# Where tiles lie in a partition: permanent tiles and weights at the upper end, the down projection's moving operands behind the tokens' tiles

## The chip, the cores and the metric

The kernel runs on one core of one Trainium2 chip. The metric is device time in microseconds (us) of one execution, lower is better. The kernel before has a median of 1196.31 us over 3 runs (1194.72 to 1197.14).

A core has five engines that run side by side. TensorE (PE) multiplies matrices: it loads a 128x128 *stationary* operand into its array (a weight load, "PEld" in the profile) and then streams a *moving* operand of up to 512 columns past it (a matmul, "PE"). VectorE (DVE) and ScalarE (ACT) do elementwise work, GpSimd (POOL) a few memsets, SyncE (SP) issues the transfers (DMA). All of them work on the on-chip memory SBUF: 128 partitions, each a line of bytes. A tile of 128x512 float32 takes 2,048 bytes of every partition. Matmul results go to a second memory, PSUM, in banks of 512 float32.

## The reference

Two layers of a token trunk, 512 tokens of width 1024. Each layer adds a mixer's output and then a gated MLP with a causal convolution of width 3. What matters here is the size and the order of the products:

```python
for i in range(DEPTH):                                  # 2 layers
    h = rms_norm(x, attn_norm[i])
    proj = h @ w_in[i]                                  # differential attention, then GLA
    mix = diff_attention(...) if i % 2 == 0 else gla_attention(...)
    cross = memory_cross_attention(mem_q, mem, ...)     # into 256 memory tokens
    x = x + concat([mix, cross]) @ w_out[i]
    h = rms_norm(x, ffn_norm[i])
    x = x + conv_ffn(h, w_up[i], conv_w[i], conv_b[i], w_down[i])

def conv_ffn(h, w_up, conv_w, conv_b, w_down):
    u = h @ w_up                                        # 1024 -> 5632
    c = causal_depthwise_conv(u, conv_w) + conv_b
    a, g = split(c, 2)
    return (silu(g) * a) @ w_down                       # 2816 -> 1024
```

## The kernel before, in words

**Products.** Every large product is done in three float32r matmuls: an operand is split into a high part and a low part, and high x high, high x low and low x high are summed in one PSUM bank. Two helpers do this. `gemm` (lines 244 to 264, matmuls on lines 255 to 257) makes tokens-by-features results: the tokens' tiles are stationary, the *weights* are the moving operand, 512 columns at a time (272 and 256 for two of the pieces). `product` (lines 267 to 274, matmuls on lines 272 to 274) makes features-by-tokens results: 128 columns of the weights are stationary and the *tokens'* tile of 512 columns is the moving operand. The output projection, the up projection and the down projection go through `product`. With a call to each matmul there is one weight load; it runs while the matmul before it streams.

**Order.** The order on PE is the program's own (line 141: the PE part of the schedule is manual). The other engines' orders come from the framework's planner, which also places every semaphore. Products of the projections are cut into units and handed out between the attention's steps by the `Filler` class, by estimated cost. Weights arrive through `make_piece` (line 214): a transfer of up to 128x1024 float32 into a `raw` tile, then ACT copies it to `whi` and DVE subtracts it into `wlo`.

**The MLP.** `ffn` (lines 1011 to 1078) works in two halves of 12 and 10 groups of 128 channels. For each group: the up projection of both gate sides (`up`, line 1018) into PSUM banks "mm" and "sm", a scaling into one of four tiles `u` (line 1026), three convolution steps into a tile `cvo` (lines 1028 to 1030), a gate, and a split into a high and a low tile (lines 1058 to 1061). The first 5 groups of a half put these two tiles among the tokens' tiles (`xs`), the other 7 or 5 into slots of their own with the tag "mid" (18 slots), called `midh` and `midl` in the profile. The down projection (lines 1066 to 1076) then runs `product` over all groups of the half, once for each of eight blocks of 128 output channels, into banks "lg" and "tp". Its moving operands are thus five pairs of `xs` tiles, then seven (or five) pairs of `mid` tiles.

**Pools and places.** Tiles come from pools. A pool takes one stretch of the partition, its size rounded to 32 bytes; with no side named, pools stack upward from the lower end, and a pool that is closed gives its stretch to the next one. A tile that reuses bytes waits until the readers of the tile before it are done. From the program before, in bytes of a partition:

| pool | holds | from | to |
| --- | --- | --- | --- |
| (reserved) | scratch of the transfers, four constants | 0 | 16,512 |
| `perm` | constants, norm gains, memory keys and values | 16,512 | 31,112 |
| `xs` | 36 slots of 2,048: tokens' tiles and most temporaries | 31,136 | 104,864 |
| `wp` | 3 slots `raw`, 5 `whi`, 5 `wlo`, 4,096 each | 104,864 | 158,112 |
| `cp` | small vectors, 64 bytes a slot | 158,112 | 162,208 |
| `at0` | layer 0's attention | 162,208 | 207,264 |
| `ff0`, `ff1` | `rB`, `u`, `cvo`, then the 18 `mid` slots from 184,864 on | 162,208 | 221,728 |
| `at1` | layer 1's attention | 162,208 | 228,128 |

`at0`, `ff0`, `at1` and `ff1` follow one another on the same bytes. Lines 135 to 138 open the permanent pools, lines 1082 and 1091 the four that alternate.

Of the kernel before, what the change touches and what calls it, by code (L numbers as in the profile page):

```python
# [129 lines left out]
def trunk(ctx, tc, head_d, x_t, mem_t, wpack, cols_a_d, cols_d, conv_d, gate_d, rel_bias, diff_lambda, consts, onehot, out):  # L130
# [1 line left out]
    mm = nc.tensor.matmul  # L132
    V, A, G = nc.vector, nc.scalar, nc.gpsimd

    perm = ctx.enter_context(tc.tile_pool(name="perm", bufs=1))
    xs = ctx.enter_context(tc.tile_pool(name="xs", bufs=1))
    wp = ctx.enter_context(tc.tile_pool(name="wp", bufs=2))
    cp = ctx.enter_context(tc.tile_pool(name="cp", bufs=4))
    ps = ctx.enter_context(tc.tile_pool(name="ps", bufs=2, space=PSUM))
    dr = ctx.enter_context(tc.tile_pool(name="dr", bufs=1, space=DRAM))  # L140
    ctx.enter_context(tc.manual_schedule(engines={mybir.EngineType.PE}))
# [1 line left out]
    def bank(tag):  # L143
        return ps.tile([128, 512], F32, name=f"ps_{tag}", tag=tag)

    def xtile():
        return xs.tile([128, S], F32, name="xt", tag="xs", bufs=XS)

    def split_tiles(pool=None, tag="xs", bufs=XS):
        pool = pool or xs  # L150
        return (pool.tile([128, S], F32R, name=tag + "h", tag=tag, bufs=bufs),
                pool.tile([128, S], F32R, name=tag + "l", tag=tag, bufs=bufs))
# [19 lines left out]
    def tables(name):  # L172
        tc.keep_in_program_order(A.preload_act_table_set(name))


    def newton(v, y, t):
        V.tensor_mul(t, y, y)
        V.scalar_tensor_tensor(t, t, -0.5, v, op0=ALU.mult, op1=ALU.mult)
        V.scalar_tensor_tensor(y, t, 1.5, y, op0=ALU.add, op1=ALU.mult)
# [48 lines left out]
    def weights(key):  # L228
        i = used[0]
        assert plan[i][0] == key, (plan[i][0], key)  # L230
        while len(made) < min(i + 2, len(plan)):
            make_piece()
        used[0] += 1
        parts, made[i] = made[i], None
        return parts
# [31 lines left out]
    def product(p, parts, n, pairs, ids=None):  # L267
        ids = range(len(parts)) if ids is None else ids
        first, last = (ids[0], ids[-1]) if len(ids) == len(parts) else (0, len(parts) - 1)
        for i in ids:  # L270
            (hi, lo), (bh, bl) = parts[i], pairs[i]
            mm(p, hi[:, blk(n)], bh, start=i == first, stop=False)  # L272
            mm(p, hi[:, blk(n)], bl, start=False, stop=False)  # L273
            mm(p, lo[:, blk(n)], bh, start=False, stop=i == last)  # L274
# [84 lines left out]
    with tc.tile_pool(name="ini", bufs=1) as ip, tc.manual_schedule(engines={E.Activation, E.DVE, E.Pool, E.SP}):  # L359
# [29 lines left out]
        parts, acc, split_w = [], [None], [None]  # L389
# [587 lines left out]
    def update(n, p, gain, acc):  # L977
        V.tensor_add(xT[n], xT[n], p)
        if gain is None:
            return  # L980
        xh[n], xl[n] = split_tiles()
        split(xh[n], xl[n], xT[n], gain(n))
        squares(xT[n], acc)


    def out_proj(l, mix, part, acc, late=None):
        got, kk = {}, dict(PASS[l][part])
        turns = cycle(("mm", "mm", "sm", "sm") if late is not None else ("mm", "sm") if acc else ("mm",))

        def unit(n, i):  # L990
            c, ks = n // 2, kk[n // 2]
            if i == 0:
                if c not in got:
                    got[c] = weights(("o", l, part, c))
                got["p", n] = bank(next(turns))
            p = got["p", n]
            product(p, got[c], n % 2, [mix[k] for k in ks], (i,))
            if i == len(ks) - 1:
                update(n, p, None if acc is None else (lambda k: c_ffn(l, k)), acc)

        def give(units):
            for u in units:
                F.add(0.65, lambda u=u: unit(*u))
        units = [(2 * c + n, i) for c, ks in PASS[l][part] for n in range(2) for i in range(len(ks))]
        if late is None:
            return give(units)
        early = [u for u in units if u[0] < 4 and kk[u[0] // 2][u[1]] != late]
        give([u for u in early if u[0] < 3])
        return lambda: give([u for u in early if u[0] == 3] + [u for u in units if u not in early])

    def ffn(pool, l, acc):
        rB = pool.tile([128, S], F32, name="rB", bufs=1)
        us = [pool.tile([128, S + 2], F32, name=f"u{i}", bufs=1) for i in range(4)]
        for u in us:
            G.memset(u[:, 0:2], 0.0)
        nu = [0]

        def up(parts, n):
            i = nu[0]
            nu[0] += 1  # L1020
            p = bank("mm" if i % 4 < 2 else "sm")
            product(p, parts, n, list(zip(xh, xl)))
            return p, us[i % 4]

        def conv(p, u, j):
            V.tensor_mul(u[:, 2:], p, rB)  # L1026
            c = pool.tile([128, S], F32, name="cvo", bufs=6)
            A.activation(c, u[:, 2:], AF.Identity, scale=cv[l][:, 2, j:j + 1], bias=cv[l][:, 3, j:j + 1])  # L1028
            V.scalar_tensor_tensor(c, u[:, 1:S + 1], cv[l][:, 1, j:j + 1], c, op0=ALU.mult, op1=ALU.add)  # L1029
            V.scalar_tensor_tensor(c, u[:, 0:S], cv[l][:, 0, j:j + 1], c, op0=ALU.mult, op1=ALU.add)  # L1030
            return c

        def row_scales(sq):
            p = bank("tp")
            mm(p, ones, sq, start=True, stop=True)
            v, t = xtile(), xtile()
            A.activation(rB, p, AF.Ln, scale=1.0 / D, bias=eps)
            V.tensor_scalar(v, p, 1.0 / D, EPS, op0=ALU.mult, op1=ALU.add)
            A.activation(rB, rB, AF.Exp, scale=-0.5)
            newton(v, rB, t)  # L1040

        base = 0
        for half, nq in enumerate(HALVES):
            mids = []
            for q in range(base, base + nq):
                wa = weights(("ua", l, q))
                wg = None
                for n in range(2):
                    ua = up(wa, n)
                    wg = wg or weights(("ug", l, q))  # L1050
                    if q == 0 and n == 0:
                        row_scales(acc[0])
                    ug = up(wg, n)
                    ca = conv(*ua, 2 * q + n)
                    cg = conv(*ug, 22 + 2 * q + n)
                    A.activation(cg, cg, AF.Silu)
                    V.tensor_mul(ca, ca, cg)
                    mh, ml = split_tiles() if len(mids) < 5 else split_tiles(pool, "mid", 18)
                    A.copy(mh, ca)
                    V.tensor_sub(ml, ca, mh.bitcast(F32))  # L1060
                    mids.append((mh, ml))
            last = half == 1
            if last and l == 0:
                tables("natural_log_exp_and_others")
            acc2 = [None]
            for c in range(4):
                pn = bank("lg"), bank("tp")
                parts = weights(("dn", l, base, c))
                for n in range(2):
                    product(pn[n], parts, n, mids)  # L1070
                for n in range(2):
                    update(2 * c + n, pn[n], (lambda k: c_attn(1, k)) if last and l == 0 else None, acc2)
                    if last and l == 0:
                        nc.sync.dma_start(xres[2 * c + n], xT[2 * c + n])
                    if last and l == 1:
                        nc.sync.dma_start(out[2 * c + n], xT[2 * c + n])
            base += nq
        return acc2

    acc = None  # L1080
    for l in range(2):
        with tc.tile_pool(name=f"at{l}", bufs=2) as pool:
            mix = [None] * 8
            sums, acc = acc, [None]
            if l == 0:
                diff_layer(pool, mix, acc)
            else:
                gla_layer(pool, mix, sums)
                out_proj(1, mix, len(PASS[1]) - 1, acc)
                F.flush()  # L1090
        with tc.tile_pool(name=f"ff{l}", bufs=2) as pool:
            acc = ffn(pool, l, acc)


def _constants():
# [72 lines left out]
```

## Time and profile before

| what | value |
| --- | --- |
| median of 3 runs (lowest, highest) | 1196.31 us (1194.72, 1197.14) |
| the profiled execution's own time | 1194.47 us |
| its span, first to last instruction | 1192.7 us |
| outside the span | 1.8 us |
| granted TensorE clock | 1.00 |
| ACT busy, DVE busy | 548.3 us, 760.1 us |
| DMA, mean over the span | 99 GB/s |

How to read it: a line of the grouped view gives the source line, the engine, the operation, the tile that is written, an arrow, and the tiles that are read; then the shapes, how many there were, their busy time together and the mean time of one in nanoseconds, and at last the idle time of the engine in front of them. For a matmul the first tile after the arrow is the moving operand and the second the stationary one. Matmuls are pipelined: one lasts longer than the distance to the next one's start, so the time that a matmul costs is the distance between starts, not its length. In a row of windows the count behind PE takes in matmuls that began before the window and still ran; the count behind PEld is that of the weight loads, one for each matmul begun.

### The profile page before, as it was taken

The numbers are of one execution on the slowest core, as the hardware profiler recorded it, in microseconds if no ns is written. First come the engines' busy times: TensorE is split into PE (matmuls) and PEld (weight loads), VectorE is DVE, ScalarE is ACT, GpSimd is POOL, SyncE is SP. The second block draws the span as 40 slices with busy tenths as digits, with TensorE's granted clock in tenths as the row PEclk, the third lists the DMA queues.
The fourth block names the chain that finished last, engine by engine and source line by source line (L and its number), as shares of the span: only waits on it lengthen the run. The fifth ranks groups of instructions, "written<-read, shape, count | busy, mean of one in ns | idle before, by whom it ended". The sixth has DMA issues, their size and how long they took to land.

```text
span 1192.7 us, 14774 instructions
## 1 busy us (share of the span) xinstructions
PE 1179.3 (99%) x5656; PEld 965.8 (81%) x5656; DVE 760.1 (64%) x1270; ACT 548.3 (46%) x966; POOL 4.5 (0%) x25
## 2 busy tenths in 40 slices
PE   9999998999999999999999999999999999999998
PEld 6887776788888888888888788987888888888887
DVE  7566587687767434767556746768777743476741
ACT  6676586564434223434436534436443422243420
POOL 0000000000000000000000000000000000000000
PEclk9999999999999999999999999999999999999999
DMA  8322214042322332322342221333233233242231
GB/s 296 124 96 81 80 55 141 27 136 76 116 96 86 109 107 71 123 71 89 117 144 78 72 71 58 103 104 125 73 109 103 81 114 106 71 124 72 89 115 44
DMA packets 39268, 117.81 MB, mean 99 GB/s; under 512 B 4671, under 2 KB 6520, under 8 KB 39198
## 3 DMA queue, kind: packets, MB, share of 16 engines
q1 hardware_dynamic: 39054, 116.62, 30.5%
q8 instruction: 44, 0.72, 0.3%
q10 hardware_dynamic: 144, 0.26, 0.1%
q14 instruction: 26, 0.21, 0.1%
HBM read 112.65 MB, written 4.21 MB: 98 GB/s over the span
## 4 chain that ended last, share of the span: by engine, by line
PE 93%; DVE 3%; ACT 2%; DMA 1%; issue 1%; SPq 0%; ACTq 0%; DVEq 0%
PE ps_mm L273 8%; PE ps_mm L274 8%; PE ps_mm L272 8%; PE ps_sm L274 7%; PE ps_sm L273 7%; PE ps_sm L272 7%; PE ps_mm L255 5%; PE ps_mm L257 5%; PE ps_mm L256 5%; PE ps_lg L273 3%; PE ps_lg L272 3%; PE ps_lg L274 3%; PE ps_tp L272 3%; PE ps_tp L273 3%; PE ps_tp L274 3%; PE ps_tp L170 2%
## 5 line engine op out<-in xcount | busy, mean ns | idle before, releaser
L201 ACT CAST whi<-raw 128x1024 fp32r<-128x1024 f32 (+4 forms) x212 | 208.5, 985 | 263.9 <-PE ps_tp L273 134.7
L204 DVE TENSOR_TENSOR wlo<-raw,whi 128x1024 fp32r<-128x1024 f32 (+4 forms) x212 | 241.3, 1140 | 117.1 <-ACT whi L201 116.4
L272 PE MATMUL ps_mm<-xsh,whi 128*128 128x512 f32 x446 | 176.4, 396 | 0.0
L273 PE MATMUL ps_mm<-xsl,whi 128*128 128x512 f32 x446 | 173.8, 390 | 0.2 <-DVE xsl L239 0.2
L274 PE MATMUL ps_mm<-xsh,wlo 128*128 128x512 f32 x446 | 173.7, 389 | 0.0
L272 PE MATMUL ps_sm<-xsh,whi 128*128 128x512 f32 x386 | 150.3, 389 | 0.0
L274 PE MATMUL ps_sm<-xsh,wlo 128*128 128x512 f32 x386 | 150.2, 389 | 0.0
L273 PE MATMUL ps_sm<-xsl,whi 128*128 128x512 f32 x386 | 150.2, 389 | 0.0
L255 PE MATMUL ps_mm<-whi,xsh 128*128 128x512 f32 (+2 forms) x352 | 136.9, 389 | 0.1
L257 PE MATMUL ps_mm<-whi,xsl 128*128 128x512 f32 (+2 forms) x352 | 131.1, 373 | 0.3 <-DVE xsl L239 0.3
L256 PE MATMUL ps_mm<-wlo,xsh 128*128 128x512 f32 (+2 forms) x352 | 130.6, 371 | 0.0
L1028 ACT ACTIVATE cvo<-u,cv 128x512 f32<-128x512 f32 x88 | 71.6, 814 | 121.4 <-DVE u L1026 121.4
L273 PEld LDWEIGHTS ps_mm<-xsl,whi 128*128 128x128 f32 x446 | 83.8, 188 | 17.8 <-DVE xsl L239 0.6
L272 PEld LDWEIGHTS ps_mm<-xsh,whi 128*128 128x128 f32 x446 | 83.8, 188 | 17.5 <-issue 0.8
L274 PEld LDWEIGHTS ps_mm<-xsh,wlo 128*128 128x128 f32 x446 | 83.7, 188 | 17.4
L1029 DVE SCALAR_TENSOR_TENSOR cvo<-u,cv,cvo 128x512 f32<-128x512 f32 x88 | 65.8, 748 | 38.7 <-ACT cvo L1028 38.7
L273 PEld LDWEIGHTS ps_sm<-xsl,whi 128*128 128x128 f32 x386 | 72.5, 188 | 15.1
L272 PEld LDWEIGHTS ps_sm<-xsh,whi 128*128 128x128 f32 x386 | 72.5, 188 | 15.0
L274 PEld LDWEIGHTS ps_sm<-xsh,wlo 128*128 128x128 f32 x386 | 72.5, 188 | 15.0
L255 PEld LDWEIGHTS ps_mm<-whi,xsh 128*128 128x128 f32 x352 | 66.3, 188 | 13.8 <-issue 3.4
L257 PEld LDWEIGHTS ps_mm<-whi,xsl 128*128 128x128 f32 x352 | 66.1, 188 | 12.6 <-DVE xsl L239 0.5
L256 PEld LDWEIGHTS ps_mm<-wlo,xsh 128*128 128x128 f32 x352 | 66.4, 189 | 9.7
(257 smaller groups left out, 1734.9 us busy)
## 6 DMA issues: line engine op xcount, KB each, us to landing
raw<-in_wpack_dram SPq DMA_DIRECT2D x178, 512.0 KB, 3.5
xt<-in_x_t_dram SPq DMA_DIRECT2D x15, 256.0 KB, 5.9
raw<-in_wpack_dram SPq DMA_DIRECT2D x15, 256.0 KB, 2.6
raw<-in_wpack_dram SPq DMA_DIRECT2D x8, 384.0 KB, 3.4
xres<-xt SPq DMA_DIRECT2D x8, 256.0 KB, 2.0
xt<-xres SPq DMA_DIRECT2D x8, 256.0 KB, 3.9
out_dram<-xt SPq DMA_DIRECT2D x8, 256.0 KB, 2.0
bt<-bias_d SPq DMA_DIRECT2D x6, 256.0 KB, 3.1
```

The source lines that it names most:

```text
L170: nc.tensor.transpose(dst, src, ident[:n, :n])
L201: ins = A.copy(hi[:, c], raw[:, c])
L204: V.tensor_sub(lo[:, c], raw[:, c], hi[:, c].bitcast(F32))
L255: mm(p, sh[k][:, blk(b)], hi, start=k == 0, stop=False)
L256: mm(p, sh[k][:, blk(b)], lo, start=False, stop=False)
L257: mm(p, sl[k][:, blk(b)], hi, start=False, stop=k == KT - 1)
L272: mm(p, hi[:, blk(n)], bh, start=i == first, stop=False)
L273: mm(p, hi[:, blk(n)], bl, start=False, stop=False)
L274: mm(p, lo[:, blk(n)], bh, start=False, stop=i == last)
L1028: A.activation(c, u[:, 2:], AF.Identity, scale=cv[l][:, 2, j:j + 1], bias=cv[l][:, 3, j:j + 1])
L1029: V.scalar_tensor_tensor(c, u[:, 1:S + 1], cv[l][:, 1, j:j + 1], c, op0=ALU.mult, op1=ALU.add)
```

## The change

The pools `perm`, `wp` and `cp` are opened on the right side: they stack downward from the upper end of the partition. `xs` and the attention's pools stay on the left. The MLP's pool is divided: the `mid` slots get a pool of their own on the left, the rest (`rB`, `u`, `cvo`) a pool on the right. No instruction is added, removed or put in another place of the program.

```diff
-    perm = ctx.enter_context(tc.tile_pool(name="perm", bufs=1))
+    perm = ctx.enter_context(tc.tile_pool(name="perm", bufs=1, side="right"))
     xs = ctx.enter_context(tc.tile_pool(name="xs", bufs=1))
-    wp = ctx.enter_context(tc.tile_pool(name="wp", bufs=2))
-    cp = ctx.enter_context(tc.tile_pool(name="cp", bufs=4))
+    wp = ctx.enter_context(tc.tile_pool(name="wp", bufs=2, side="right"))
+    cp = ctx.enter_context(tc.tile_pool(name="cp", bufs=4, side="right"))
...
-    def ffn(pool, l, acc):
+    def ffn(mid, pool, l, acc):
...
-                    mh, ml = split_tiles() if len(mids) < 5 else split_tiles(pool, "mid", 18)
+                    mh, ml = split_tiles() if len(mids) < 5 else split_tiles(mid, "mid", 18)
...
-        with tc.tile_pool(name=f"ff{l}", bufs=2) as pool:
-            acc = ffn(pool, l, acc)
+        with tc.tile_pool(name=f"mid{l}", bufs=2) as mid, tc.tile_pool(name=f"ff{l}", bufs=2, side="right") as pool:
+            acc = ffn(mid, pool, l, acc)
```

## The prediction

> **What bounds the kernel now.** I read the page first, then who waits for whom on PE, then the matmuls by form, then the distances between their starts in chosen stretches.
>
> ```profile
> span 1192.7 us, 14774 instructions
> ...
> PE 1179.3 (99%) x5656; PEld 965.8 (81%) x5656; DVE 760.1 (64%) x1270; ACT 548.3 (46%) x966; POOL 4.5 (0%) x25
> ...
> PEclk9999999999999999999999999999999999999999
> ...
> PE 93%; DVE 3%; ACT 2%; DMA 1%; issue 1%; SPq 0%; ACTq 0%; DVEq 0%
> ```
>
> PE is busy for 1179.3 of 1192.7 us at the full granted clock; DVE and ACT have a third and a half of the span free. 13.4 us of PE idle time are all that an earlier start of anything could win. Where they lie, by the view of waits of PE:
>
> ```profile
> PE ps_sm L640 <- DVE o L649: 2.2, 1, 2.2
> PE ps_tp L368 <- POOL idle L365: 1.3, 1, 1.3
> ...
> PE ps_mm L257 <- DVE xsl L239: 0.3, 1, 0.3
> ...
> PE ps_sm L346 <- DVE xt L340: 0.2, 1, 0.2
> PE ps_mm L273 <- DVE xsl L239: 0.2, 1, 0.2
> ```
>
> The largest are in layer 0's attention and in the warm-up. At the seams between attention and MLP, where a pool takes over another's bytes, only the last three stand, 0.3, 0.2 and 0.2 us, and they wait for tokens' tiles being split or squared. So the reuse of bytes that this change rearranges costs PE nothing today, and taking it away wins nothing. If the change moves the time, it is through the rate at which PE runs. The groups by form:
>
> ```profile
> L272 PE MATMUL ps_mm<-xsh,whi 128*128 128x512 f32 x446 | 176.4, 396 | 0.0
> L272 PE MATMUL ps_sm<-xsh,whi 128*128 128x512 f32 x386 | 150.3, 389 | 0.0
> L255 PE MATMUL ps_mm<-whi,xsh 128*128 128x512 f32 x288 | 117.9, 409 | 0.0
> L274 PE MATMUL ps_lg<-midh,wlo 128*128 128x512 f32 x96 | 38.0, 395 | 0.0
> L272 PE MATMUL ps_tp<-midh,whi 128*128 128x512 f32 x96 | 37.9, 395 | 0.0
> L272 PE MATMUL ps_tp<-xsh,whi 128*128 128x512 f32 x80 | 31.3, 391 | 0.0
> L274 PE MATMUL ps_lg<-xsh,wlo 128*128 128x512 f32 x80 | 31.1, 389 | 0.0
> ```
>
> The same matmul, in the same bank and against the same weights, lasts 389 to 391 ns with a tokens' tile as the moving operand and 395 ns with a `mid` tile. What it costs shows in the distance of the starts. Four stretches without idle time (columns: stretch, its length, then busy time and count for PE, PEld, DVE, ACT, POOL, then clock and DMA):
>
> ```profile
> 390.85:394.25 3.40, 3.40 (x17) 2.82 (x15) 3.02 (x5) 1.77 (x2) 0.00 (x0) 1.00 0.50 160
> 394.94:398.44 3.50, 3.50 (x17) 2.81 (x15) 1.39 (x2) 0.97 (x2) 0.00 (x0) 1.00 0.28 115
> 399.14:402.57 3.43, 3.43 (x17) 2.82 (x15) 0.69 (x1) 0.67 (x1) 0.00 (x0) 1.00 0.02 5
> 689.31:699.96 10.65, 10.65 (x49) 8.82 (x47) 3.67 (x3) 5.38 (x8) 0.00 (x0) 1.00 0.22 59
> ```
>
> The first is the down projection over tokens' tiles: 15 starts in 3.40 us, **226.7 ns** each. The second is the same product three tiles further on, over `mid`: 15 in 3.50 us, **233.3 ns**. The third is tokens' tiles again, right behind `mid`: 228.7 ns, so the pace takes a few matmuls to settle. The fourth is `gemm`, where weights move: 47 in 10.65 us, 226.6 ns. ACT and DVE do no more in the second stretch than in the first, and the clock is 1.00 in all four. What differs is where the moving tile lies. The starts themselves:
>
> ```profile
> 393.57 0.39 PE L272 MATMUL ps_lg<-xsh,whi 128*128 128x512 f32 x1
> 393.79 0.39 PE L273 MATMUL ps_lg<-xsl,whi 128*128 128x512 f32 x1
> 394.02 0.39 PE L274 MATMUL ps_lg<-xsh,wlo 128*128 128x512 f32 x1
> 394.25 0.40 PE L272 MATMUL ps_lg<-midh,whi 128*128 128x512 f32 x1
> 394.48 0.39 PE L273 MATMUL ps_lg<-midl,whi 128*128 128x512 f32 x1
> 394.70 0.40 PE L274 MATMUL ps_lg<-midh,wlo 128*128 128x512 f32 x1
> 394.94 0.39 PE L272 MATMUL ps_lg<-midh,whi 128*128 128x512 f32 x1
> 395.17 0.40 PE L273 MATMUL ps_lg<-midl,whi 128*128 128x512 f32 x1
> 395.41 0.39 PE L274 MATMUL ps_lg<-midh,wlo 128*128 128x512 f32 x1
> 395.64 0.40 PE L272 MATMUL ps_lg<-midh,whi 128*128 128x512 f32 x1
> ```
>
> The lengths turn from an even 0.39 to 0.39 and 0.40 by turns with the first `mid` matmul, and nothing waits there. This is a steady property of the operand, not a stall.
>
> **The change part by part.** It adds and removes no instruction and moves none, so there is no issue, transfer or queue to cost. What it does is give every tile another address, and other neighbours in time.
>
> *Addresses.* `xs` drops to the end of the reserved bytes, 16,512. The `mid` slots begin 36 x 2,048 bytes later, at 90,240, so they lie at the same place as `xs` modulo 2,048. `perm` (14,624 with rounding), `wp` and `cp` go to the upper end, then `rB`, `u`, `cvo` below them. Two readings fit the rows. By *distance*: `mid` lies from 184,864 on, every fast moving tile below 158,112. By *offset*: modulo 512, `xs` and the weights both lie at 416 (31,136 and 117,152), `mid` at 32. After the change `xs` and `mid` lie at 128, and the weights at 224 if the upper end is a multiple of 512 (14,624 below it).
>
> *The `mid` matmuls.* 96 in each of six groups, 576. By distance they join `xs` outright; by offset they share whatever pace `xs` gets. At 226.7 ns they win 576 x 6.67 ns = 3.8 us. The tokens' matmuls behind them lose their 2.0 ns: 15 in each of some 28 stretches (7 of the 8 blocks in 2 halves of 2 layers), 0.8 us. Together **-4.6 us**. From below the bound is no gain: `mid` stays at 233.3.
>
> *The tokens' matmuls in `product`* (446 and 386 on each of three lines, and the 80s: 3 x 832 + 6 x 80 = 2,976) keep their neighbours but get another offset. No row shows offset 128. The nearest rows are the two paces above, 6.67 ns apart. I take no change, the value of the pace that four groups of five show; the bounds are one such step up and one down, 2,976 x 6.67 = 19.8 us each way.
>
> *Weights as the moving operand*: 3 x 288 = 864 matmuls. They move up to where `mid` was, so by distance they would take over its pace, 864 x 6.67 = **+5.8 us**; by offset 224 is as unknown as 128. I take nothing, because weights and `mid` need not share a cause, and keep +5.8 as a rival.
>
> *Reuse of bytes.* `mid0` now lies on `at0`'s bytes and `at1` on `mid0`'s. The first writer of layer 1's attention tiles is ACT's copy out of the first `gemm`'s bank, which follows the last down projection on PE in any case, so its wait for the readers of `mid0` ends first. `ff0` meets `at0` only in its lowest 544 bytes (`rB` against the end of the second `o`, read for the last time before the output projection ends). `ff1` meets `at1`'s `gs`, `qx`, `kd`, `st` and `go`, whose last reader is the gate, before the last output projection; PE has that projection as cover, longer than any of the waits above. I cost this at nothing. Were a cover gone, ACT's first copy would hold up the bank and with it the next unit on PE, as in the waits of 0.2 to 2.2 us. The planner may order ACT and DVE a little differently; the same rows bound that to about 1 us either way.
>
> *Sum.* 1194.5 us (the profiled execution: 1192.7 and 1.8 around it) - 4.6 = 1189.9. The runs' median lies 1.8 above that execution, so for the median 1196.3 - 4.6 = **1191.7 us**.
>
> **The rivals.** *One step faster for all of `product`.* 226.7 is 34 times 6.67 and 233.3 is 35 times, so the pace seems to come in steps; the `xs` and `mid` tiles now begin on a multiple of 128 bytes, which no moving tile did before. At 33 steps (220.0 ns) the 2,976 win 19.8 us and the 576 win 7.7, with 0.8 for settling 28.3: **1168 us**. For it speaks the step, against it that no row shows 220. The Trainium skill ("TensorE: Matmul & The Clock Gate", Part 2, back-to-back issue gap) puts the distance at N/2.4 + 2.5, about 216 ns for 512 columns; no large product of this trace runs so fast, and if the new place brought it, an estimate by that page is 3,552 x 10.9 = 39 us less.
>
> *All of `product` one step slower.* Moving and stationary operand lay at the same offset (416 and 416) wherever the pace was 226.7, and 128 bytes apart (32 and 416) where it was 233.3. If it is this relation that counts, moving `perm` alone breaks it: tokens at 128, weights at 224, 96 apart. Then 2,976 matmuls go to 233.3 and `mid` stays: +19.8, **1216 us**, and with `gemm`, whose relation is broken too, 1222. It decides as soon as a third of `product` is struck: 992 x 6.67 = 6.6 us outweigh the 4.6. For it speaks that it explains every stretch above; against it that distance does so as well.
>
> *Only the moving weights slower*: +5.8 - 4.6 = +1.2, **1197.5 us**.
>
> *Nothing.* The place is not the cause, and `mid` is slow for another reason, say because it is read in a long row: **1196.3 us**. The Trainium skill speaks for this one ("SBUF — State Buffer", Who interferes with whom): PE never waits for another user of SBUF, and weight load and moving operand have ports of their own. The stretch over `mid` speaks against it: 6.67 ns more each with nothing else changed.
>
> **How the numbers follow.** The forecast 0.35; one step faster 0.14; all of `product` slower 0.31; only the weights slower 0.10; nothing 0.10. Faster by over 0.2% (2.4 us, about what a measurement of this kernel can tell from no change) are the first two, 0.49. Within 0.2% fall "nothing" and a third of "only the weights", 0.13. Slower is the rest, 0.38. The likeliest case alone would be 1189 to 1195. The range must hold both signs: from the step faster, 1168, to the step slower, 1217, which leaves out those that strike `gemm` too or win more than one step.
>
> **What would show it.** In the profile after: the `midh` and `midl` groups at 389 ns as the tokens' groups are (forecast), or tokens' groups at 395 with lengths by turns (slower rival), or all below 389 (faster rival); the moving weights of L255 to L257 at 226.6 ns a start or near 233; the seams' waits still at 0.2 to 0.3 us. The forecast is wrong if the stretch over tokens' tiles in the up projection no longer runs at 226.7, whatever `mid` does.

## The result and the profile after

| | median us (lowest, highest, runs) | span of the profiled execution, us |
| --- | --- | --- |
| before | 1196.41 (1194.72, 1197.14, 4) | 1192.7 |
| after | 1213.63 (1213.15, 1215.58, 4) | 1211.4 |

The kernel became slower: the ratio of after to before is 1.0149, with a 95% interval of 1.0131 to 1.0167. The profiled execution of after took 1213.15 us, which is 1.8 us more than its span, as before.

The page of after, its span, its busy times and the granted clock:

```profile
span 1211.4 us, 14774 instructions
...
PE 1198.2 (99%) x5656; PEld 965.5 (80%) x5656; DVE 760.6 (63%) x1270; ACT 547.7 (45%) x966; POOL 4.6 (0%) x25
...
PEclk9999999999999999999999999999999999999999
```

The span has grown by 18.7 us and PE's busy time by 18.9. No instruction was added, the clock is full, and the other engines are where they were within 0.6 us. So PE does not wait for more, it works for longer. The view of PE's waits after (tile and line that waited, releaser, us in total, times, longest) confirms it:

```profile
PE ps_sm L640 <- DVE o L649: 2.2, 1, 2.2
PE ps_tp L368 <- POOL idle L365: 1.3, 1, 1.3
...
PE ps_mm L257 <- DVE xsl L239: 0.3, 1, 0.3
...
PE ps_sm L346 <- DVE xt L340: 0.2, 1, 0.2
PE ps_mm L273 <- DVE xsl L239: 0.2, 1, 0.2
```

These are the same waits, to the tenth of a microsecond. The groups of matmuls by form, after:

```profile
L272 PE MATMUL ps_mm<-xsh,whi 128*128 128x512 f32 x446 | 178.8, 401 | 0.0
...
L272 PE MATMUL ps_sm<-xsh,whi 128*128 128x512 f32 x386 | 152.5, 395 | 0.0
...
L255 PE MATMUL ps_mm<-whi,xsh 128*128 128x512 f32 x288 | 118.2, 410 | 0.0
...
L272 PE MATMUL ps_tp<-midh,whi 128*128 128x512 f32 x96 | 37.9, 395 | 0.0
...
L274 PE MATMUL ps_lg<-midh,wlo 128*128 128x512 f32 x96 | 37.9, 395 | 0.0
...
L272 PE MATMUL ps_lg<-xsh,whi 128*128 128x512 f32 x80 | 31.6, 395 | 0.0
L274 PE MATMUL ps_lg<-xsh,wlo 128*128 128x512 f32 x80 | 31.6, 395 | 0.0
```

Before, a matmul of `product` lasted 389 to 391 ns with a tokens' tile and 395 with a `mid` tile. Now both kinds last 395: the tokens' matmuls have taken over the slow pace of `mid`, where the forecast had `mid` take over theirs. The first group (396 ns before, 401 now) is no exception: in both traces 23 of its 446 matmuls last over 450 ns, up to 0.80 us, and raise its mean; the others went from 389 to 395. The moving weights on L255 have hardly moved, 409 to 410.

The same four stretches as in the prediction, cut at the same matmuls, are tokens' tiles, `mid`, tokens' tiles right behind `mid`, and `gemm` (columns: stretch, length, busy time and count of PE, PEld, DVE, ACT, POOL, then clock and DMA):

```profile
395.66:399.16 3.50, 3.50 (x16) 2.81 (x15) 3.06 (x4) 1.76 (x2) 0.00 (x0) 1.00 0.54 164
399.86:403.36 3.50, 3.50 (x16) 2.81 (x15) 1.39 (x2) 0.86 (x2) 0.00 (x0) 1.00 0.24 95
404.06:407.56 3.50, 3.50 (x16) 2.81 (x15) 0.69 (x1) 0.69 (x1) 0.00 (x0) 1.00 0.02 5
698.64:709.40 10.76, 10.76 (x49) 8.83 (x48) 3.68 (x3) 5.46 (x8) 0.00 (x0) 1.00 0.25 65
```

Tokens' tiles took 3.40 us for 15 starts before and take 3.50 now, `mid` 3.50 as before, tokens' tiles behind `mid` 3.43 and now 3.50; `gemm`'s 47 went from 10.65 to 10.76 us. The border between tokens' and `mid` tiles can no longer be seen in the starts:

```profile
398.46 0.39 PE L272 MATMUL ps_lg<-xsh,whi 128*128 128x512 f32 x1
398.70 0.39 PE L273 MATMUL ps_lg<-xsl,whi 128*128 128x512 f32 x1
398.93 0.39 PE L274 MATMUL ps_lg<-xsh,wlo 128*128 128x512 f32 x1
399.16 0.39 PE L272 MATMUL ps_lg<-midh,whi 128*128 128x512 f32 x1
399.40 0.39 PE L273 MATMUL ps_lg<-midl,whi 128*128 128x512 f32 x1
399.63 0.39 PE L274 MATMUL ps_lg<-midh,wlo 128*128 128x512 f32 x1
```

Over the whole execution, from the starts in the trace (the distance from one matmul of 512 columns to the next, those above 300 ns left out): tokens' tiles in `product`, 2,927 distances, mean 227.07 ns before and 233.32 after; `mid`, some 570, 233.06 and 233.56; moving weights in `gemm`, 752, 228.90 and 229.62. The first is 2,927 x 6.25 = 18.3 us, the others 0.3 and 0.5: together 19.1, against 18.7 of the span. The cost is spread over all matmuls of `product` and has no place of its own in the timeline.

### The profile page after: what moved, and what is told of

Same layout as the page of the kernel before. It is cut to its first block, busy times and chain, and to the rows that moved or that the text cites. A ratio compares the mean times of both kernels' runs of the same rounds, so it can differ in the third digit from the quotient of the medians.

```text
span 1211.4 us, 14774 instructions
## 1 busy us (share of the span) xinstructions
PE 1198.2 (99%) x5656; PEld 965.5 (80%) x5656; DVE 760.6 (63%) x1270; ACT 547.7 (45%) x966; POOL 4.6 (0%) x25
## 4 chain that ended last, share of the span: by engine, by line
PE 92%; DVE 4%; ACT 2%; DMA 1%; issue 1%; SPq 0%; ACTq 0%; DVEq 0%
PE ps_mm L273 9%; PE ps_mm L272 8%; PE ps_mm L274 8%; PE ps_sm L273 7%; PE ps_sm L272 7%; PE ps_sm L274 7%; PE ps_mm L255 5%; PE ps_mm L257 5%; PE ps_mm L256 5%; PE ps_lg L273 3%; PE ps_lg L274 3%; PE ps_lg L272 3%; PE ps_tp L273 3%; PE ps_tp L272 3%; PE ps_tp L274 3%; PE ps_tp L170 2%
## 5 line engine op out<-in xcount | busy, mean ns | idle before, releaser
L272 PE MATMUL ps_mm<-xsh,whi 128*128 128x512 f32 x446 | 178.8, 401 | 0.0
L273 PE MATMUL ps_mm<-xsl,whi 128*128 128x512 f32 x446 | 176.2, 395 | 0.2 <-DVE xsl L239 0.2
L274 PE MATMUL ps_mm<-xsh,wlo 128*128 128x512 f32 x446 | 176.1, 395 | 0.0
L272 PE MATMUL ps_sm<-xsh,whi 128*128 128x512 f32 x386 | 152.5, 395 | 0.0
L274 PE MATMUL ps_sm<-xsh,wlo 128*128 128x512 f32 x386 | 152.4, 395 | 0.0
L273 PE MATMUL ps_sm<-xsl,whi 128*128 128x512 f32 x386 | 152.4, 395 | 0.0
L255 PE MATMUL ps_mm<-whi,xsh 128*128 128x512 f32 (+2 forms) x352 | 137.1, 390 | 0.1
L273 PEld LDWEIGHTS ps_mm<-xsl,whi 128*128 128x128 f32 x446 | 83.7, 188 | 20.5 <-DVE xsl L239 0.6
L272 PEld LDWEIGHTS ps_mm<-xsh,whi 128*128 128x128 f32 x446 | 83.7, 188 | 20.3 <-issue 0.8
L274 PEld LDWEIGHTS ps_mm<-xsh,wlo 128*128 128x128 f32 x446 | 83.7, 188 | 20.3
L272 PEld LDWEIGHTS ps_sm<-xsh,whi 128*128 128x128 f32 x386 | 72.4, 188 | 17.7
L273 PEld LDWEIGHTS ps_sm<-xsl,whi 128*128 128x128 f32 x386 | 72.4, 188 | 17.7
L274 PEld LDWEIGHTS ps_sm<-xsh,wlo 128*128 128x128 f32 x386 | 72.4, 188 | 17.6
L255 PEld LDWEIGHTS ps_mm<-whi,xsh 128*128 128x128 f32 x352 | 66.2, 188 | 13.8 <-issue 3.4
```

The source lines that it names most:

```text
L255: mm(p, sh[k][:, blk(b)], hi, start=k == 0, stop=False)
```

## The experiments

Why should a matmul run slower because its operands lie elsewhere? There are three theories, each about the place of the moving operand:

- *Relation*: what counts is how far the moving and the stationary operand are apart, modulo some power of two. From the changed program: the upper end at which tiles stack is 229,344; `perm` starts at 214,720 and the first `whi` slot at 173,760, which is 192 modulo 256, as are all slots of `whi` and `wlo`. The tokens' and `mid` tiles (from 16,512 and 90,240 on) are at 128. Moving less stationary is thus -64 in `product` and +64 in `gemm`. Before, it was 0 for the tokens' tiles and 128 for `mid`.
- *Own offset*: the moving operand's own place modulo 512 counts: 416 is good, 128 and 32 are bad, whatever the weights do.
- *Distance*: operands far up in the partition are slow.

Each experiment adds an unused tile of a few bytes, so that what lies behind it in its pool, and the pools stacked behind that one, shift; no instruction changes. "Lower" and "higher" are the direction in which it shifts. Where a line was added, the matmuls of `product` stand on L273 to L275 (in one case L274 to L276) instead of L272 to L274. The runs were made in three groups, each beside the kernel before, which took 1196.53 us in the group of the first four runs below, 1194.86 in that of 128, 320 and 32 bytes and of `wlo`, and 1197.78 (one run) in that of 96, 160 and 224 bytes and of `whi`; differences of up to 3 us between runs of different groups say nothing.

### The weights, 64 bytes

The changed kernel with relation 0 again. The weights, and with them the small vectors and the MLP's `rB`, `u` and `cvo`, lie 64 bytes lower; tokens' and `mid` tiles stay:

```diff
+    perm.tile([128, 16], F32, name="pad")
     C = perm.tile(...)
```

> The changed kernel with 64 unused bytes at the top of perm, so that weights, small vectors and the MLP's tiles lie 64 bytes lower: the stationary weights then lie at 128 modulo 512, as the tokens' and mid tiles do. Theory 'relation' (the pace hangs on the offset of the moving operand against the stationary one, 0 being good): product at 226.7 ns a start for tokens and mid alike, tokens' groups at 389 ns, about 4.6 us below the kernel before: 1191.7 us. Theory 'own offset' (the moving operand's own place modulo 512, 128 being bad): as the changed kernel, 1213.6 us. Theory 'distance' (weights or moving tiles far up are slow): as the changed kernel, 1213.6 us.

Measured: 1192.20 us, 0.9965 of before (0.9951 to 0.9979). The stretches cut at the same matmuls:

```profile
391.97:395.37 3.40, 3.40 (x16) 2.81 (x15) 3.03 (x5) 1.77 (x2) 0.00 (x0) 1.00 0.51 158
396.05:399.45 3.40, 3.40 (x16) 2.82 (x15) 1.39 (x2) 0.99 (x2) 0.00 (x0) 1.00 0.32 129
400.13:403.53 3.40, 3.40 (x16) 2.81 (x15) 0.69 (x1) 0.66 (x1) 0.00 (x0) 1.00 0.02 5
688.69:699.34 10.65, 10.65 (x48) 8.82 (x47) 3.68 (x3) 5.38 (x8) 0.00 (x0) 1.00 0.19 60
```

All three stretches of the down projection, `mid` too, are at 3.40 us. 64 bytes take back the whole loss and bring the gain that was forecast. The moving operands of `product` lie exactly where they lay in the slow kernel, at 128 modulo 512, so their own offset is not the cause; and the weights are still far up in the partition, stationary in `product` and moving in `gemm`, and both run at the fast pace, so distance isn't either.

The counterpart: the kernel before, with 64 bytes put in between the tokens' tiles and the weights (a pool opened between `xs` and `wp`), which makes relation -64 at the old places:

```diff
     xs = ctx.enter_context(tc.tile_pool(name="xs", bufs=1))
+    gap = ctx.enter_context(tc.tile_pool(name="gap", bufs=1))
...
+    gap.tile([128, 16], F32, name="pad")
```

> The kernel before with 64 unused bytes between xs and wp: weights and all above them move up by 64, tokens' tiles stay at 416. Moving minus stationary is then -64 for tokens in product and +64 in gemm, as in the changed kernel; mid against weights stays at +128. 'Relation': tokens in product at 233.3 ns, gemm unchanged within 1 ns, about 18 us slower than before: 1214 us. 'Own offset': product unchanged, 1196.4 us (gemm's moving weights at 480 instead of 416 could cost up to 864 x 6.67 ns = 5.8 us). 'Distance': 1196.4 us.

Measured: 1213.52 us, 1.0139 (1.0124 to 1.0154): the whole loss of the change, without the change. Tokens, `mid` and `gemm` in its stretches:

```profile
395.24:398.74 3.50, 3.50 (x17) 2.81 (x15) 3.07 (x4) 1.77 (x2) 0.00 (x0) 1.00 0.53 159
399.43:402.91 3.48, 3.48 (x16) 2.82 (x15) 1.39 (x2) 0.86 (x2) 0.00 (x0) 1.00 0.27 109
...
697.81:708.57 10.76, 10.76 (x48) 8.83 (x47) 3.67 (x3) 5.38 (x8) 0.00 (x0) 1.00 0.27 64
```

### `mid` alone, and everything together

In the kernel before, `mid` moved by 384 bytes, from 184,864 to 185,248, which is 416 modulo 512 like the weights (`cvo`, which no matmul reads, moves with it):

```diff
         nu = [0]
+        pool.tile([128, 96], F32, name="pad", bufs=1)
```

> The kernel before with 384 unused bytes in the MLP's pool ahead of the mid slots, so that only mid moves, to 416 modulo 512, where tokens' tiles and weights lie. 'Relation' and 'own offset': mid at 226.7 ns and 389 ns long, 1191.7 us. 'Distance' (mid lies as far up as before, from 185,248 on): mid stays at 233.3 ns, 1196.4 us.

Measured: 1191.33 us, 0.9961 (0.9945 to 0.9976). Two groups of `mid`, and the stretch over `mid`:

```profile
L272 PE MATMUL ps_tp<-midh,whi 128*128 128x512 f32 x96 | 37.3, 389 | 0.0
...
L274 PE MATMUL ps_tp<-midh,wlo 128*128 128x512 f32 x96 | 37.3, 389 | 0.0
```

```profile
394.85:398.25 3.40, 3.40 (x16) 2.82 (x15) 1.39 (x2) 0.99 (x2) 0.00 (x0) 1.00 0.32 127
```

395 ns became 389 although `mid` lies higher than before: distance falls a second time. Then everything moved up by 224 bytes, so that tokens' tiles and weights are at 128 modulo 512 both, with `mid` still 128 off:

```diff
+    perm.tile([128, 56], F32, name="pad")
     C = perm.tile(...)
```

> The kernel before with 224 unused bytes at the start, so that tokens' tiles lie at 128 modulo 512 as in the changed kernel, and the weights at 128 with them; mid at 256. All differences are those of the kernel before. 'Relation': nothing changes, 1196.4 us, tokens at 226.7 and mid at 233.3 ns. 'Own offset': tokens in product at 233.3 ns, about 18 us slower, 1214 us. 'Distance': 1196.4 us.

Measured: 1196.52 us, 0.9996 (0.9987 to 1.0005), no change. A tokens' and a `mid` group:

```profile
L273 PE MATMUL ps_sm<-xsh,whi 128*128 128x512 f32 x386 | 150.3, 389 | 0.0
...
L274 PE MATMUL ps_lg<-midl,whi 128*128 128x512 f32 x96 | 38.0, 396 | 0.0
```

Of the three theories only the relation gives all four results.

### Which relations are good

The rest of the offsets, all with the changed kernel and another size of the pad in `perm`, 320 bytes for instance:

```diff
+    perm.tile([128, 80], F32, name="pad")
     C = perm.tile(...)
```

320 bytes make the two places differ by -256 in `product`; if the relation counts modulo 256, this is as good as 0.

> The changed kernel with 320 unused bytes at the top, so that moving and stationary operand lie 256 apart modulo 512 in both helpers. 'The relation counts modulo 256': as with no difference, 226.7 ns and 1192 us. 'It counts modulo 512 or more': 256 is a difference like any other, product near 233 ns, 1213 us.

Measured: 1192.45 us, 0.9977 (0.9967 to 0.9986).

```profile
L273 PE MATMUL ps_sm<-xsh,whi 128*128 128x512 f32 x386 | 150.3, 389 | 0.0
```

Modulo 256, then. The modulus isn't smaller, since 128 is bad (`mid` before). Next the relation +64 in `product` and -64 in `gemm`, that is, the changed kernel's two relations exchanged:

> The changed kernel with 128 unused bytes at the top, so that in product the moving operand lies 64 above the stationary one modulo 512 (+64), in gemm 64 below (-64): the signs of the changed kernel turned round. 'Any difference hurts': product near 233 ns, 1213 us, as the changed kernel. 'Only the moving operand lying below hurts': product near 227 ns and gemm's 864 matmuls near 233 ns, 1192 + 5.8 = 1198 us.

Measured: 1203.34 us, 1.0066 (1.0051 to 1.0081), which neither expectation gave. The groups of one product, by line, and the stretches of tokens' tiles (those behind `mid`) and `gemm`:

```profile
L273 PE MATMUL ps_sm<-xsh,whi 128*128 128x512 f32 x386 | 152.1, 394 | 0.0
L275 PE MATMUL ps_sm<-xsh,wlo 128*128 128x512 f32 x386 | 151.3, 392 | 0.0
L274 PE MATMUL ps_sm<-xsl,whi 128*128 128x512 f32 x386 | 149.9, 388 | 0.0
```

```profile
404.42:407.85 3.43, 3.43 (x16) 2.82 (x15) 0.69 (x1) 0.67 (x1) 0.00 (x0) 1.00 0.02 5
...
694.93:705.89 10.96, 10.96 (x48) 8.84 (x47) 3.68 (x3) 5.61 (x8) 0.00 (x0) 1.00 0.24 70
```

`product` now costs a third of a step (3.43 us for 15, 228.9 ns each) and `gemm` a whole one (10.96 us for 47, 233.2 ns). So -64 is bad in either helper, and `gemm` came off lightly in the changed kernel because it stood at the mild side, +64. By the starts in the trace, against the version with 64 bytes: tokens 2,927 x 2.13 = 6.2, `mid` 570 x 2.2 = 1.3, `gemm` 752 x 4.64 = 3.5, together 11.0, against 10.8 us between the two profiled spans (1200.8 and 1190.0).

Half of the smallest change so far, 32 bytes:

> The changed kernel with 32 unused bytes at the top: -32 in product, +32 in gemm. 'Any difference hurts by a whole step': near 233 ns in product, 1213 us. 'The cost grows with the difference': half a step or less, 229 to 231 ns, 1199 to 1206 us. 'Only differences of 64 and more count': 226.7 ns, 1192 us.

Measured: 1216.67 us, 1.0180 (1.0163 to 1.0197).

```profile
398.64:402.14 3.50, 3.50 (x16) 2.82 (x15) 3.06 (x4) 1.77 (x2) 0.00 (x0) 1.00 0.60 163
...
701.69:712.66 10.97, 10.97 (x48) 8.81 (x47) 3.67 (x3) 5.57 (x8) 0.00 (x0) 1.00 0.25 64
```

Both helpers are slow by a whole step, so the cost does not grow with the difference. Three more pads had one run each, and were also meant to find out whether some place is better than 34 steps:

> The changed kernel with 96 unused bytes at the top: moving against stationary +32 in product, -32 in gemm, modulo 256. Theory 'relation modulo 256, no difference is the only good place': product near 233 ns (35 steps), gemm near 233 ns: 1216 us as at -32. Theory 'a moving operand that lies a little above is harmless': product 227 to 229 ns, 1192 to 1203 us.

> The changed kernel with 160 unused bytes at the top: +96 in product, -96 in gemm. 'No difference is the only good place': product near 233 ns, 1213 to 1217 us. 'There is a place better than no difference' (33 steps, 220 ns): 1192 - 3552 x 6.67 ns = 1168 us.

> The changed kernel with 224 unused bytes at the top: -96 in product (160 modulo 256), +96 in gemm. 'No difference is the only good place': product near 233 ns, 1213 to 1217 us. 'There is a place better than no difference': 1168 us.

Measured 1216.73, 1218.69 and 1220.63 us. All of it stands in one table, by the mean distance of starts of matmuls of 512 columns (34 steps of 6.667 ns are 226.7 ns, 35 are 233.3); the last three times are from the slowest of the three groups:

| relation in `product` / `gemm`, modulo 256 | where | `product` over tokens, ns | `gemm`, ns | us |
| --- | --- | --- | --- | --- |
| 0 / 0 | 64 bytes | 226.84 | 228.62 | 1192.20 |
| 0 / 0 | 320 bytes | 226.84 | 228.77 | 1192.45 |
| +64 / -64 | 128 bytes | 228.97 | 233.26 | 1203.34 |
| -64 / +64 | the change | 233.32 | 229.62 | 1213.63 |
| -32 / +32 | 32 bytes | 233.30 | 233.12 | 1216.67 |
| +32 / -32 | 96 bytes | 233.33 | 233.04 | 1216.73 |
| +96 / -96 | 160 bytes | 233.33 | 233.91 | 1218.69 |
| -96 / +96 | 224 bytes | 234.24 | 233.60 | 1220.63 |

With `mid` before the change (128, 233.06 ns) these are all eight multiples of 32. One is free, +64 costs a third of a step in `product` and 1.0 ns in `gemm`, and the others cost about a whole step. For 512 columns none is better than 0.

For 256 columns that does not hold. `gemm`'s one piece of that width gives 84 distances in each trace. They have a mean of 119.7 to 119.8 ns in all five traces with relation 0, 116.2 and 117.8 in the two with +64, and 114.4 with 128 bytes of pad (-64), a slow place for the wide matmuls; all other relations lie in between, and none is above relation 0. This is too little to show in the times (96 matmuls, half a microsecond), but the good place depends on the width.

### Which of the two stationary operands collides

While a matmul streams, the next one's weights are loaded (after the change PEld is busy for 80% of the span beside PE's 99%). So the moving operand could collide with the weights that are being loaded *beside* it, or with its *own*, which were loaded before. `product` takes `whi`, `whi`, `wlo`, and the two slots can be moved apart: in the kernel before, 64 bytes between the `whi` and the `wlo` slots, and in another run 64 bytes ahead of `whi` and 192 behind it, so that `wlo` keeps its relation.

```diff
-                split_w[0] = [wp.tile([128, WTILE], F32R, name=n, tag=n, bufs=WB) for n in ("whi", "wlo")]
+                hi = wp.tile([128, WTILE], F32R, name="whi", tag="whi", bufs=WB)
+                if k == 0:
+                    wp.tile([128, 16], F32, name="pad", bufs=1)
+                lo = wp.tile([128, WTILE], F32R, name="wlo", tag="wlo", bufs=WB)
+                split_w[0] = [hi, lo]
```

> The kernel before with 64 unused bytes between the whi and the wlo slots, so that wlo alone lies 64 higher and tokens lie at -64 against wlo, at 0 against whi. In product each tile gives three matmuls, L272 and L273 on whi, L274 on wlo; the weight load that runs beside L272 is whi's, beside L273 wlo's, beside L274 the next whi's. Theory 'the load beside it': only L273 is struck in itself, a third of product. Theory 'its own stationary operand': only L274. If a struck matmul costs one step of 6.67 ns: (832 + 160) x 6.67 = 6.6 us, about 1203 us in both; if phases carry over, up to 18 us, 1214. The lengths of the three lines in the up projection (389 each before) tell which one is longer.

> The kernel before with 64 unused bytes ahead of the whi slots and 192 behind them, so that whi lies 64 higher and wlo at the old place modulo 256: the counterpart of the run with wlo moved. Tokens lie at -64 against whi, at 0 against wlo. 'The load beside it': whi's loads run beside L274 and L272, so the starts behind these two are late and L273's is not. 'Its own stationary operand': L272 and L273 are late, L274 is not. 'Phases carry over', so that lines can't be told apart: the three together come to a whole number of steps (102 before, 104 with wlo moved), 103 to 105, without a clear good line. Time between 1203 and 1214 us.

Measured 1207.16 and 1211.58 us, one run each, 12.3 and 13.8 us above the kernel before in their groups. The second run moves `whi` by 64 bytes and everything behind it by 256, so by nothing modulo 256; that `product` is slow there too takes the small vectors and the MLP's tiles, which moved with the weights in the earlier runs, out of the question. The same product by line, first with `wlo` moved, then with `whi` moved:

```profile
L274 PE MATMUL ps_sm<-xsh,wlo 128*128 128x512 f32 x386 | 153.4, 397 | 0.0
L273 PE MATMUL ps_sm<-xsl,whi 128*128 128x512 f32 x386 | 151.3, 392 | 0.0
L272 PE MATMUL ps_sm<-xsh,whi 128*128 128x512 f32 x386 | 150.3, 389 | 0.0
```

```profile
L273 PE MATMUL ps_sm<-xsl,whi 128*128 128x512 f32 x386 | 153.4, 397 | 0.0
L274 PE MATMUL ps_sm<-xsh,wlo 128*128 128x512 f32 x386 | 152.1, 394 | 0.0
L272 PE MATMUL ps_sm<-xsh,whi 128*128 128x512 f32 x386 | 149.9, 388 | 0.0
```

With `wlo` moved, L274, the only line that uses it, suffers most, which speaks for *own*. With `whi` moved, L272 should suffer by either theory, and it doesn't; L273 and L274 do. The three lines together take 104 steps in both runs, against 102 before, although one line of three is struck by either theory in the first and two in the second. `gemm` fits neither theory: all its stationary tiles lie at one place modulo 256, and its moving weights stand at relation 0 or +64 in these two runs. Each alone is cheap (228.6 and 229.6 ns in the table), yet mixed they take 231.9 and 232.9 ns. So the cost of a matmul is not a function of its own relation alone; what its neighbours do counts too. Which reads meet, or whether reads meet at all, stays open; only that the relation of the operands decides is shown.

## Why the prediction was wrong

**No waits to win**: right. The idle time of PE was 13.4 us and is 13.2 (1211.4 - 1198.2), with the same waits.

**Reuse of bytes costs nothing**: right, by the waits at the seams, which are still 0.3, 0.2 and 0.2 us.

**The tokens' matmuls in `product`**: this is the step that failed; the prediction put their change at nothing: "I take no change, the value of the pace that four groups of five show; the bounds are one such step up and one down, 2,976 x 6.67 = 19.8 us each way." They became slower by 6.25 ns each, 18.3 us, close to the upper bound of one step. The choice between the bounds counted groups, but four of the five groups were fast for a single reason, that tokens' tiles and weights happened to lie at the same place modulo 256. They were one observation, and the change removed exactly the condition that they shared. Working out the addresses of both operands, which the prediction did, was the right step; to take the pace of a relation that would exist nowhere after the change was the wrong one. A relation other than 0 had one row, `mid`, and it was slow.

**The `mid` matmuls, -4.6 us**: the tie between tokens and `mid` was seen rightly, both now have one pace, but they met at the slow one, so nothing came. The size was right where the relation is 0: moving `mid` alone gives a ratio of 0.9961, which is 4.7 us, and the change with 64 bytes 0.9965, 4.2 us.

**The moving weights at nothing**: nearly right in size, 752 x 0.72 = 0.5 us, but by luck of place. At -64, where `gemm` stood in the run with 128 bytes, the same weights cost 3.5 us.

**The addresses**: the prediction had the weights at 224 if the upper end is a multiple of 512. The end lies 32 bytes below such a multiple, the weights are at 192, and the relation is -64 instead of -96. That left `gemm` nearly unharmed; with -96 and +96 in the table the time is 1220.63 us. For the same reason `ff0` and `at0` share 576 bytes and not 544, which changes nothing in the waits.

**The rivals**: "All of `product` one step slower", 1216 us, is what happened, for the reason given there. It was 2.4 us too high, mostly for two reasons: the tokens' mean before was already 227.07 and not 226.7 ns (18.3 us instead of 19.8), and the medians lie 17.2 us apart where the profiled spans lie 18.7. By the prediction's own measure it wins once a third of `product` is struck, and all of it was. Its evidence fitted distance as well, and that, by the prediction's words, spoke against it; its chance stood at 0.31. "One step faster" falls: no relation tried brought `product` below 226.8 ns. "Only the moving weights slower" falls for this change, where they cost 0.5 us. "Nothing" falls: 64 bytes of pad are worth about 21 us. The Trainium skill ("SBUF — State Buffer", Who interferes with whom) gives the moving operand and the weight load independent ports. The runs here don't contradict that there are two ports, but independence by itself gives no reason why the stretch over tokens' tiles takes 3.50 us in the changed kernel and 3.40 us with the weights 64 bytes lower.

**What to run instead**: the change with 64 bytes of pad (1192.20 us), or the kernel before with 384 bytes ahead of `mid` (1191.33 us). Both beat the kernel before by about 0.4%. The gain is that of `mid`, not of the new arrangement.

## What to carry to other kernels

Before tiles are moved, work out where moving and stationary operand of every large product lie modulo 256 bytes, before and after; in this kernel a move of pools that looked free cost every float32r matmul of `product` over tokens' tiles about a thirty-fourth of its time, and 64 bytes of pad decided it. Measure it for the width at hand, since 256 columns behaved otherwise here. Where all good rows share a condition, they are one piece of evidence; ask whether the change keeps it. And where a change is meant to move one group, move that group alone first: here a pad of 384 bytes had the whole gain.

## What the runs showed of the hardware that was not expected

The paces of matmuls of 512 columns look like a grid. With relation 0, 3,392 of 3,498 distances in `product` are 226 or 227 ns (the version with 64 bytes), and 15 of them make 3.40 us; in the changed kernel none of 3,500 is, all but a few lie between 230 and 236 with a mean of 233.36, and 15 make 3.50 us. The difference over 15 starts, 0.10 us, is 6.67 ns each, so that the two paces are 34 and 35 such steps. The three matmuls of one tile in `product` together take whole numbers of steps at most places: 102 at relation 0, 103 at +64, 104 with one of the two slots moved, 105 in the changed kernel; at -96 they take 105.4, so the grid is not the whole account. In the kernel before, the distances over `mid` turned between 229 and 238 ns, and over the tokens' tiles behind it they needed a few matmuls to come back to 226.7, which is why the stretch there had 3.43 us. What sets the step, and how one matmul's lateness is handed to the next, was not tried.
